# Gated linear attention in a hybrid decoder layer: score and state products of each head over its own 64 rows

## The chip, the cores and the metric

The kernel runs on one core of one Trainium2 chip. The metric is device time in microseconds (us) of one execution, as the median over runs; lower is better. TensorE multiplies matrices and writes its results to the PSUM banks, VectorE, ScalarE and GpSimd work element by element, and SyncE issues the transfers.

## What is computed

One layer over 4096 positions of width 1024, in fp32. Three groups of token mixers read the same normalised input: a gated linear recurrence (RG-LRU), gated linear attention (GLA) and a cross-attention into 256 memory tokens. Their outputs are gated with SiLU, multiplied by one output projection, added to the input and normalised. The change is in GLA alone, which has 4 heads with a key width of 64 and a value width of 128:

```python
q_dec = q * jnp.exp(cum)
k_dec = k * jnp.exp(-cum)
att = jnp.einsum("bnihk,bnjhk->bnhij", q_dec, k_dec)
att = jnp.where(causal, att, 0.0)
o_intra = jnp.einsum("bnhij,bnjhv->bnihv", att, v)
kv = jnp.einsum("bnjhk,bnjhv->nbhkv", k * jnp.exp(cum_last - cum), v)
decay = jnp.exp(cum_last[:, :, 0]).transpose(1, 0, 2, 3)
# state <- decay * state + kv, from chunk to chunk
o_inter = jnp.einsum("bnihk,nbhkv->bnihv", q_dec, s_prev)
o = (o_intra + o_inter)   # then an RMS norm per head
```

## The kernel before

The first part of the kernel goes through the sequence in 4 blocks of 1024 positions, each of two units of 512. Within a block a list gives the order of the groups of weights: `V0+G0 Q0 L0 L1 X0 L2 L3 X1 L4 V1 G1 Q1 ...`. L are RG-LRU groups, X cross-attention heads, and V, G and Q the values, gates and queries/keys of a pair of GLA heads. A second part does the output projection.

Each group issues its projections (`proj`, lines 118 to 124, with `mm3` in lines 74 to 77: three fp32r matmuls for each of 8 slices) and hands what comes after them to a generator. After each projection `tick` lets every active generator go on by one stage, in the order in which they were spawned. So the small matmuls of a generator stand between the large ones of the projections, and the order of the program on TensorE is that of these ticks.

The two heads of a pair share the 128 partitions: rows 0 to 63 belong to one, 64 to 127 to the other. `GlaQ.unit` (line 549) writes the decayed queries to `qz` with one VectorE instruction per head (line 561). `qz` has a slot of 128 columns per chunk and head, whose other 64 rows stay at the zeros written at the start (line 223). `GlaQ.post` then has, for each unit of 512 positions as 4 chunks of 128, these stages:

1. `kd`, the decayed keys (line 575), and an empty stage.
2. `pk`: four transposes of `kd`, copied to `kt_` by ScalarE (lines 587 to 591). Then `att(0)`: the scores of chunks 0 and 1 into one `pa` bank, each a matmul of 128 rows by 256 columns (both heads, line 583), and two masked copies to `attm` by VectorE (line 585).
3. `att(1)` for chunks 2 and 3, then `pkv`, the products of keys and values. These have 64 columns of weights per head and write 64 partitions each (line 599). `advance` makes the states of chunks 1 to 3 (lines 605 and 606).
4. For each half `c2` (chunks 0 and 1, then 2 and 3) one `po` bank: for each chunk and head the state product over 128 rows of `qz` (line 616) and the score product over 128 rows of `attm` (line 617). After the first half `advance(3)` writes the state for the next unit. ScalarE squares the bank (line 622), VectorE sums (624), GpSimd makes the factor (lines 69 and 71), and VectorE multiplies (626).
5. `pt`: eight transposes of the result, multiplied by the gate (lines 631 and 634).

All of these small tiles (`pk`, `pa`, `pkv`, `po`, `pt`, and those of L and X) come from the tag `aux` of the pool `ps`, four PSUM banks (lines 54 and 55). Stage 4 of a block's first unit and stage 2 of its second fall into the same tick.

Of the kernel before, what the change touches and what calls it, by code (L numbers as in the profile page):

```python
# [9 lines left out]
F32 = mybir.dt.float32  # L10
F32R = mybir.dt.float32r
BF16 = mybir.dt.bfloat16
U32 = mybir.dt.uint32
AF = mybir.ActivationFunctionType
ALU = mybir.AluOpType
# [4 lines left out]
P = 128  # L20
# [16 lines left out]
def hybrid_layer(ctx: ExitStack, tc: tile.TileContext, x, x_t, mem, mem_t, final_g,  # L37
                 w_lru, w_v0, w_oth, w_g2, w_mem, w_out, prm, out):
    nc = tc.nc
# [11 lines left out]
    def acc(name):  # L51
        return ps.tile([P, 512], F32, tag="acc", name=name)

    def aux(name):
        return ps.tile([P, 512], F32, tag="aux", name=name)
# [10 lines left out]
    def rstd_of(ss, n, cols, tag, eng=None):  # L66

        ms = small.tile([P, cols], F32, tag=tag + "m", name=tag + "m")
        (eng or nc.gpsimd).tensor_scalar(out=ms, in0=ss, scalar1=1.0 / n, scalar2=EPS, op0=ALU.mult, op1=ALU.add)
        r = small.tile([P, cols], F32, tag=tag + "r", name=tag + "r")  # L70
        nc.gpsimd.tensor_tensor(out=r, in0=ms, in1=mhalf[:, :cols], op=ALU.pow)
        return r
# [10 lines left out]
    c1 = p1.enter_context(tc.tile_pool(name="c1", bufs=1))  # L83
# [14 lines left out]
    def spawn(g):  # L98
        active.append(g)

    def big(tag, dt=F32):
        return wk.tile([P, BLK], dt, tag=tag, name=tag)
# [15 lines left out]
    def proj(o, wg, i, h, n=UNIT):  # L118

        hi, lo = wg  # L120
        hh, hl = h
        for kt in range(KT):
            s = slice(kt * P, (kt + 1) * P)
            mm3(o, hi[:, i, s], lo[:, i, s], hh[:, kt, :n], hl[:, kt, :n], kt == 0, kt == KT - 1)
# [88 lines left out]
    cmask = c1.tile([P, P], F32, name="cmask")  # L213
    make_upper_triangular(nc, cmask)
    attm = []
    for i in range(4):
        t = c1.tile([P, 2, P], F32, name=f"attm{i}")
        nc.gpsimd.memset(t, 0.0)
        attm.append(t)
    qzt = []  # L220
    for i in range(2):
        t = c1.tile([P, 4, 2, P], F32, name=f"qz{i}")
        nc.gpsimd.memset(t, 0.0)
        qzt.append(t)
    halo = cst.tile([P, 8, 3], F32, name="halo")
    nc.gpsimd.memset(halo, 0.0)
    hst = cst.tile([P, 8], F32, name="hst")
# [1 line left out]
    s_st = []  # L229
    for p in range(2):  # L230
        t = c1.tile([P, P], F32, name=f"s_st{p}")
# [54 lines left out]
    def usl(u):  # L286
        return slice(u * UNIT, (u + 1) * UNIT)

    def silu_gate(wg, i, h, sg, u):
        g = acc("gate")  # L290
        proj(g, wg, i, h)

        def post():

            nc.scalar.activation(out=sg[:, usl(u)], in_=g, func=AF.Tanh, scale=0.5)  # L295
            nc.vector.scalar_tensor_tensor(out=sg[:, usl(u)], in0=sg[:, usl(u)], scalar=1.0, in1=g,  # L296
                                           op0=ALU.add, op1=ALU.mult)
            yield 1
        spawn(post())

    def store_y(b, ct, y):
        nc.sync.dma_start(out=y_ds[b][ct], in_=y)
# [11 lines left out]
    class Lru(Group):  # L314
# [5 lines left out]
        def unit(self, u, h):  # L320
            wg = self.wg
            o = acc("u")
            proj(o, wg, 0, h)
            spawn(self.post(u, o))
            yield 1
            if self.sg is None:
                self.sg = big("sg")
            silu_gate(wg, 1, h, self.sg, u)
            yield 1
# [218 lines left out]
    class GlaQ(Group):  # L548
        def unit(self, u, h):
            g = gla[self.j]  # L550
            if "dec" not in g:
                g["dec"] = gla_decay(self.j)
            ep, em_, fs = g["dec"]
            qz = qzt[u]
            o = acc("q")
            proj(o, self.wg, 0, h)
            o3 = o.rearrange("p (s t) -> p s t", t=P)
            ep3 = ep[:, usl(u)].rearrange("p (s t) -> p s t", t=P)
            for hd in range(2):
                r = slice(hd * 64, hd * 64 + 64)  # L560
                nc.vector.scalar_tensor_tensor(out=qz[r, :, hd, :], in0=o3[r], scalar=0.125, in1=ep3[r],
                                               op0=ALU.mult, op1=ALU.mult)
            yield 1
            o = acc("k")
            proj(o, self.wg, 1, h)
            spawn(self.post(u, o))
            yield 1

        def post(self, u, o):
            p = self.j  # L570
            g = gla[p]
            ep, em_, fs = g["dec"]
            vt, sgs, qz = g["v"][u], g["sg"], qzt[u]
            kd = wk.tile([P, UNIT], F32, tag="uc", name="kd")
            nc.vector.tensor_tensor(out=kd, in0=o, in1=em_[:, usl(u)], op=ALU.mult)
            yield 1
            yield 1

            def att(c2):
                pa = aux("pa").rearrange("p (c a t) -> p c a t", c=2, a=2)  # L580
                for c in range(2):
                    s = 2 * c2 + c
                    nc.tensor.matmul(pa[:, c], kd[:, s * P:(s + 1) * P], qz[:, s], start=True, stop=True)
                for c in range(2):
                    nc.vector.copy_predicated(attm[2 * c2 + c],
                                              cmask.bitcast(U32).unsqueeze(1).broadcast_to([P, 2, P]), pa[:, c])
            pk = aux("pk")
            for s in range(4):
                nc.tensor.transpose(out=pk[:, s * P:(s + 1) * P], in_=kd[:, s * P:(s + 1) * P], identity=ident)
            kt_ = wk.tile([P, UNIT], F32, tag="t2", name="ktk")  # L590
            nc.scalar.copy(out=kt_, in_=pk)
            att(0)
            yield 1
            att(1)
            pkv = aux("pkv").rearrange("p (s d) -> p s d", d=P)
            for s in range(4):
                for hd in range(2):
                    r = slice(hd * 64, hd * 64 + 64)
                    nc.tensor.matmul(pkv[r, s, :], kt_[:, s * P + hd * 64:s * P + hd * 64 + 64],
                                     vt[:, s, hd * P:(hd + 1) * P], start=True, stop=True)  # L600
            sts = [s_st[p]] + [small.tile([P, P], F32, tag="st", name="st", bufs=3) for _ in range(3)]

            def advance(s, dst):
                sub = u * 4 + s
                nc.vector.tensor_tensor(out=dst, in0=sts[s], in1=pkv[:, s, :], op=ALU.add)
                nc.vector.tensor_scalar(out=dst, in0=dst, scalar1=fs[:, sub:sub + 1], scalar2=None, op0=ALU.mult)
            for s in range(3):
                advance(s, sts[s + 1])
            yield 1
            on = big("i").rearrange("p (a d) -> p a d", d=P)  # L610
            for c2 in range(2):
                po = aux("po").rearrange("p (a d) -> p a d", d=P)
                for c in range(2):
                    s = 2 * c2 + c
                    for hd in range(2):
                        nc.tensor.matmul(po[:, 2 * c + hd, :], qz[:, s, hd, :], sts[s], start=True, stop=False)
                        nc.tensor.matmul(po[:, 2 * c + hd, :], attm[s][:, hd, :], vt[:, s, hd * P:(hd + 1) * P],
                                         start=False, stop=True)
                if c2 == 0:
                    advance(3, s_st[p])  # L620
                sq = wk.tile([P, 4, P], F32, tag="t2", name="sq")
                nc.scalar.activation(out=sq, in_=po, func=AF.Square)
                ss = small.tile([P, 4], F32, tag="oss", name="oss")
                nc.vector.tensor_reduce(out=ss, in_=sq, op=ALU.add, axis=AX.X)
                r = rstd_of(ss, P, 4, "o")
                nc.vector.tensor_tensor(out=on[:, 4 * c2:4 * c2 + 4, :], in0=po, in1=r.unsqueeze(2).broadcast_to([P, 4, P]), op=ALU.mult)
            yield 1
            for hd in range(2):
                pt = aux("pt")
                for s in range(4):  # L630
                    nc.tensor.transpose(out=pt[:, s * P:(s + 1) * P], in_=on[:, 2 * s + hd, :],
                                        identity=ident)
                sg = sgs[hd]
                nc.vector.tensor_tensor(out=sg[:, usl(u)], in0=pt, in1=sg[:, usl(u)], op=ALU.mult)
                if u == NU - 1:
                    store_y(self.b, 8 + 2 * p + hd, sg)
            yield 1
# [283 lines left out]
    for q, (b, p, c) in enumerate(steps):  # L921
        n, _, grp, fresh = SEQ[p]
# [11 lines left out]
        for i in range(4):  # L934
            for cc in (range(NCH) if tail else [c]):
                th, tl, wh, wl = T[q - c + cc]
                for k in range(CH):
                    t = slice(i * P, (i + 1) * P)
# [78 lines left out]
```

## Time and profile before

| | us |
|---|---|
| median of 3 runs | 2636.55 |
| lowest and highest | 2634.82, 2637.12 |
| the profiled execution's own time | 2638.23 |
| its span, first to last instruction | 2636.1 |
| TensorE busy | 2581.3 (98%) |
| VectorE busy | 1686.8 (64%) |
| ScalarE busy | 1316.5 (50%) |

The profile is that of one execution. PE is TensorE's matmuls and PEld its weight loads, which run beside the matmuls; DVE is VectorE, ACT ScalarE, POOL GpSimd. A releaser (after "<-") is what ended the idle time of an engine; "issue" is idle time for which the profile shows no cause. A shape such as "128*64 128x128" is weights of 128 rows by 64 columns, then the 128 partitions by 128 columns that stream past them. The ends of matmuls are modelled and successive ones overlap, so their starts count.

### The profile page before, as it was taken

How to read it: one execution, taken by the hardware profiler on the slowest of the kernel's cores; microseconds unless marked ns; L12 is line 12 of the kernel's file. 1: busy time of each engine (PE TensorE's matmuls, PEld its weight loads, DVE VectorE, ACT ScalarE, POOL GpSimd, SP SyncE). 2: the span in 40 equal slices, each digit the busy share in tenths (PEclk: the TensorE clock that was granted, in tenths of full speed). 3: DMA queues.
4: the chain of work that ended last, by engine and by line, in shares of the span. 5: the costliest groups of instructions: out<-in, count | busy, mean ns of one | idle time of the engine just before them, and what ended most of it. 6: DMA issues, size and time to landing. Idle time of an engine off the chain costs nothing.

```text
span 2636.1 us, 33203 instructions
## 1 busy us (share of the span) xinstructions
PE 2581.3 (98%) x12954; PEld 2182.4 (83%) x12954; DVE 1686.8 (64%) x2700; ACT 1316.5 (50%) x1950; POOL 92.1 (3%) x165
## 2 busy tenths in 40 slices
PE   7999999999999999999999999999998999999997
PEld 6888888888888888888888888888887887878786
DVE  6466546665775558466546756664568587695866
ACT  6355534653664366365525744654266344353543
POOL 2000000000000000000000000000000000010100
PEclk9999999999999999999999999999999999999999
DMA  8211111331445133111212321211127456565642
GB/s 282 69 61 58 65 61 59 128 115 52 172 141 198 46 116 124 52 68 66 70 39 90 121 72 55 68 57 62 55 98 249 166 204 210 192 215 192 214 138 96
DMA packets 111597, 302.98 MB, mean 115 GB/s; under 512 B 10608, under 2 KB 11728, under 8 KB 111440
## 3 DMA queue, kind: packets, MB, share of 16 engines
q1 hardware_dynamic: 111440, 300.86, 33.5%
q8 instruction: 101, 1.65, 0.2%
q14 instruction: 56, 0.46, 0.1%
HBM read 237.91 MB, written 62.91 MB: 114 GB/s over the span
## 4 chain that ended last, share of the span: by engine, by line
PE 82%; DVE 9%; DMA 3%; ACT 3%; issue 2%; POOL 1%; SPq 0%; POOLq 0%; DVEq 0%; ACTq 0%
PE gate L75 8%; PE gate L77 8%; PE gate L76 8%; PE out L944 6%; PE out L945 6%; PE out L943 6%; PE u L77 4%; PE u L76 4%; PE u L75 4%; PE q L76 3%; PE q L75 3%; PE q L77 3%; PE vp L481 2%; PE vp L479 2%; PE vp L480 2%
## 5 line engine op out<-in xcount | busy, mean ns | idle before, releaser
L75 PE MATMUL gate<-hh,whi 128*128 128x512 f32 x1024 | 400.6, 391 | 0.0
L77 PE MATMUL gate<-hh,wlo 128*128 128x512 f32 x1024 | 398.9, 390 | 0.0
L76 PE MATMUL gate<-hl,whi 128*128 128x512 f32 x1024 | 398.6, 389 | 0.0
L943 PE MATMUL out<-wh,th 128*128 128x512 f32 x896 | 351.0, 392 | 6.8 <-ACT wh L841 6.8
L944 PE MATMUL out<-wl,th 128*128 128x512 f32 x896 | 351.4, 392 | 5.9 <-DVE wl L853 5.8
L945 PE MATMUL out<-wh,tl 128*128 128x512 f32 x896 | 350.9, 392 | 0.0
L114 DVE TENSOR_TENSOR wlo<-raw,whi 128x1024 fp32r<-128x1024 f32 (+2 forms) x152 | 191.2, 1281 | 199.8 <-ACT whi L113 170.2
L838 ACT CAST th<-B 128x1024 fp32r<-128x1024 f32 x96 | 101.1, 1053 | 281.3 <-PE out L944 281.3
L113 ACT CAST whi<-raw 128x1024 fp32r<-128x1024 f32 (+2 forms) x152 | 162.2, 1096 | 138.6 <-PE gate L76 86.5
L77 PEld LDWEIGHTS gate<-hh,wlo 128*128 128x128 f32 x1024 | 192.2, 188 | 40.4
L75 PEld LDWEIGHTS gate<-hh,whi 128*128 128x128 f32 x1024 | 192.2, 188 | 40.4 <-issue 1.5
L76 PEld LDWEIGHTS gate<-hl,whi 128*128 128x128 f32 x1024 | 192.3, 188 | 39.2
L851 DVE TENSOR_TENSOR tl<-B,th 128x1024 fp32r<-128x1024 f32 x96 | 117.5, 1224 | 144.6 <-ACT th L838 143.9
L944 PEld LDWEIGHTS out<-wl,th 128*128 128x128 f32 x896 | 169.7, 189 | 43.4 <-DVE wl L853 7.9
L943 PEld LDWEIGHTS out<-wh,th 128*128 128x128 f32 x896 | 169.6, 189 | 42.4 <-ACT wh L841 7.2
L75 PE MATMUL u<-hh,whi 128*128 128x512 f32 x512 | 203.7, 398 | 0.0
L76 PE MATMUL u<-hl,whi 128*128 128x512 f32 x512 | 199.6, 390 | 0.0
L77 PE MATMUL u<-hh,wlo 128*128 128x512 f32 x512 | 199.5, 390 | 0.0
L945 PEld LDWEIGHTS out<-wh,tl 128*128 128x128 f32 x896 | 169.6, 189 | 35.3
L337 DVE SCALAR_TENSOR_TENSOR uc<-u,prm_sb,uc 128x511 f32<-128x511 f32 (+2 forms) x192 | 143.1, 745 | 63.1 <-ACT uc L334 62.7
L296 DVE SCALAR_TENSOR_TENSOR sg<-sg,gate 128x512 f32<-128x512 f32 x128 | 86.7, 683 | 105.7 <-ACT sg L295 105.4
L295 ACT ACTIVATE sg<-gate 128x512 f32<-128x512 f32 x128 | 75.9, 600 | 152.4 <-PE gate L77 148.0
(226 smaller groups left out, 5393.0 us busy)
## 6 DMA issues: line engine op xcount, KB each, us to landing
wraw<-ws_d SPq DMA_DIRECT2D x192, 256.0 KB, 3.4
raw<-in_w_oth SPq DMA_DIRECT2D x72, 512.0 KB, 3.8
raw<-in_w_lru SPq DMA_DIRECT2D x64, 576.0 KB, 3.8
B<-y_d SPq DMA_DIRECT2D x32, 1024.0 KB, 7.3
r<-in_x SPq DMA_DIRECT2D x34, 512.0 KB, 5.2
xt<-in_x_t SPq DMA_DIRECT2D x32, 512.0 KB, 3.8
y_d<-sg SPq DMA_DIRECT2D x32, 512.0 KB, 3.2
y_d<-i SPq DMA_DIRECT2D x32, 512.0 KB, 2.6
```

Source lines behind the costliest of these rows:

```text
L75: nc.tensor.matmul(o, w_hi, r_hi, start=start, stop=False)
L76: nc.tensor.matmul(o, w_hi, r_lo, start=False, stop=False)
L77: nc.tensor.matmul(o, w_lo, r_hi, start=False, stop=stop)
L113: nc.scalar.copy(out=hi[:, i, :width], in_=raw[:, :width])
L114: nc.vector.tensor_tensor(out=lo[:, i, :width], in0=raw[:, :width], in1=hi.bitcast(F32)[:, i, :width], op=ALU.subtract)
L296: nc.vector.scalar_tensor_tensor(out=sg[:, usl(u)], in0=sg[:, usl(u)], scalar=1.0, in1=g, op0=ALU.add, op1=ALU.mult)
L337: nc.vector.scalar_tensor_tensor(out=uc[:, d:UNIT], in0=o[:, 0:UNIT - d], scalar=w, in1=uc[:, d:UNIT], op0=ALU.mult, op1=ALU.add)
L838: nc.scalar.copy(out=th, in_=t)
L851: nc.vector.tensor_tensor(out=tl, in0=t, in1=th.bitcast(F32), op=ALU.subtract)
L943: nc.tensor.matmul(o, th[:, k, t], wh[:, k], start=st, stop=False, **sk)
L944: nc.tensor.matmul(o, th[:, k, t], wl[:, k], start=False, stop=False, **sk)
L945: nc.tensor.matmul(o, tl[:, k, t], wh[:, k], start=False, stop=sp, **sk)
```

## The change

The two heads are computed over 64 rows each, and each has a bank of its own. `qz` has one slot per chunk, without zeros and without the clearing at the start, and one VectorE instruction fills it. `attm` becomes two tiles (one per head, four chunks) in place of four. All eight score products of a unit (4 chunks by 2 heads) come in one stage, each of 64 rows by 128 columns, into two `pa` banks that are held together; two masked copies follow. In the stage of `po` both banks are taken at once. For each chunk the two heads' state products, over 64 rows, come first, then the two score products over 128 rows. `advance(3)` and both heads' norms stand behind all of them.

```diff
@@ -213,15 +213,13 @@
     cmask = c1.tile([P, P], F32, name="cmask")
     make_upper_triangular(nc, cmask)
     attm = []
-    for i in range(4):
-        t = c1.tile([P, 2, P], F32, name=f"attm{i}")
+    for hd in range(2):
+        t = c1.tile([P, 4, P], F32, name=f"attm{hd}")
         nc.gpsimd.memset(t, 0.0)
         attm.append(t)
     qzt = []
     for i in range(2):
-        t = c1.tile([P, 4, 2, P], F32, name=f"qz{i}")
-        nc.gpsimd.memset(t, 0.0)
-        qzt.append(t)
+        qzt.append(c1.tile([P, 4, P], F32, name=f"qz{i}"))
     halo = cst.tile([P, 8, 3], F32, name="halo")
     nc.gpsimd.memset(halo, 0.0)
     hst = cst.tile([P, 8], F32, name="hst")
@@ -556,10 +554,7 @@
             proj(o, self.wg, 0, h)
             o3 = o.rearrange("p (s t) -> p s t", t=P)
             ep3 = ep[:, usl(u)].rearrange("p (s t) -> p s t", t=P)
-            for hd in range(2):
-                r = slice(hd * 64, hd * 64 + 64)
-                nc.vector.scalar_tensor_tensor(out=qz[r, :, hd, :], in0=o3[r], scalar=0.125, in1=ep3[r],
-                                               op0=ALU.mult, op1=ALU.mult)
+            nc.vector.scalar_tensor_tensor(out=qz, in0=o3, scalar=0.125, in1=ep3, op0=ALU.mult, op1=ALU.mult)
             yield 1
             o = acc("k")
             proj(o, self.wg, 1, h)
@@ -576,22 +571,22 @@
             yield 1
             yield 1
 
-            def att(c2):
-                pa = aux("pa").rearrange("p (c a t) -> p c a t", c=2, a=2)
-                for c in range(2):
-                    s = 2 * c2 + c
-                    nc.tensor.matmul(pa[:, c], kd[:, s * P:(s + 1) * P], qz[:, s], start=True, stop=True)
-                for c in range(2):
-                    nc.vector.copy_predicated(attm[2 * c2 + c],
-                                              cmask.bitcast(U32).unsqueeze(1).broadcast_to([P, 2, P]), pa[:, c])
+            HD = [slice(0, 64), slice(64, 128)]
             pk = aux("pk")
             for s in range(4):
                 nc.tensor.transpose(out=pk[:, s * P:(s + 1) * P], in_=kd[:, s * P:(s + 1) * P], identity=ident)
             kt_ = wk.tile([P, UNIT], F32, tag="t2", name="ktk")
             nc.scalar.copy(out=kt_, in_=pk)
-            att(0)
-            yield 1
-            att(1)
+
+            pa = [aux("pa").rearrange("p (s t) -> p s t", t=P) for _ in range(2)]
+            for s in range(4):
+                for hd in range(2):
+                    nc.tensor.matmul(pa[hd][:, s], kd[HD[hd], s * P:(s + 1) * P], qz[HD[hd], s],
+                                     start=True, stop=True)
+            for hd in range(2):
+                nc.vector.copy_predicated(attm[hd], cmask.bitcast(U32).unsqueeze(1).broadcast_to([P, 4, P]),
+                                          pa[hd])
+            yield 1
             pkv = aux("pkv").rearrange("p (s d) -> p s d", d=P)
             for s in range(4):
                 for hd in range(2):
@@ -607,28 +602,28 @@
             for s in range(3):
                 advance(s, sts[s + 1])
             yield 1
-            on = big("i").rearrange("p (a d) -> p a d", d=P)
-            for c2 in range(2):
-                po = aux("po").rearrange("p (a d) -> p a d", d=P)
-                for c in range(2):
-                    s = 2 * c2 + c
-                    for hd in range(2):
-                        nc.tensor.matmul(po[:, 2 * c + hd, :], qz[:, s, hd, :], sts[s], start=True, stop=False)
-                        nc.tensor.matmul(po[:, 2 * c + hd, :], attm[s][:, hd, :], vt[:, s, hd * P:(hd + 1) * P],
-                                         start=False, stop=True)
-                if c2 == 0:
-                    advance(3, s_st[p])
+            on = big("i").rearrange("p (h s d) -> p h s d", h=2, d=P)
+            po = [aux("po").rearrange("p (s d) -> p s d", d=P) for _ in range(2)]
+            for s in range(4):
+                for hd in range(2):
+                    nc.tensor.matmul(po[hd][:, s], qz[HD[hd], s], sts[s][HD[hd]], start=True, stop=False)
+                for hd in range(2):
+                    nc.tensor.matmul(po[hd][:, s], attm[hd][:, s], vt[:, s, hd * P:(hd + 1) * P],
+                                     start=False, stop=True)
+            advance(3, s_st[p])
+            for hd in range(2):
                 sq = wk.tile([P, 4, P], F32, tag="t2", name="sq")
-                nc.scalar.activation(out=sq, in_=po, func=AF.Square)
+                nc.scalar.activation(out=sq, in_=po[hd], func=AF.Square)
                 ss = small.tile([P, 4], F32, tag="oss", name="oss")
                 nc.vector.tensor_reduce(out=ss, in_=sq, op=ALU.add, axis=AX.X)
                 r = rstd_of(ss, P, 4, "o")
-                nc.vector.tensor_tensor(out=on[:, 4 * c2:4 * c2 + 4, :], in0=po, in1=r.unsqueeze(2).broadcast_to([P, 4, P]), op=ALU.mult)
+                nc.vector.tensor_tensor(out=on[:, hd], in0=po[hd], in1=r.unsqueeze(2).broadcast_to([P, 4, P]),
+                                        op=ALU.mult)
             yield 1
             for hd in range(2):
                 pt = aux("pt")
                 for s in range(4):
-                    nc.tensor.transpose(out=pt[:, s * P:(s + 1) * P], in_=on[:, 2 * s + hd, :],
+                    nc.tensor.transpose(out=pt[:, s * P:(s + 1) * P], in_=on[:, hd, s, :],
                                         identity=ident)
                 sg = sgs[hd]
                 nc.vector.tensor_tensor(out=sg[:, usl(u)], in0=pt, in1=sg[:, usl(u)], op=ALU.mult)
```

## Rows read from the trace of the kernel before

**Rows 1.** The page: busy time, granted clock in 40 slices, chain by engine.

```profile
PE 2581.3 (98%) x12954; PEld 2182.4 (83%) x12954; DVE 1686.8 (64%) x2700; ACT 1316.5 (50%) x1950; POOL 92.1 (3%) x165
...
PEclk9999999999999999999999999999999999999999
...
PE 82%; DVE 9%; DMA 3%; ACT 3%; issue 2%; POOL 1%; SPq 0%; POOLq 0%; DVEq 0%; ACTq 0%
```

**Rows 2.** Waits of TensorE's matmuls: us in total, times, longest us.

```profile
PE rb L169 <- POOL xr L71: 9.6, 2, 8.5
...
PE sp L415 <- DVE i L626: 1.1, 2, 0.5
```

**Rows 3.** Groups by line and shape: busy us, mean ns of one, idle before.

```profile
L616 PE MATMUL po<-st,qz 128*128 128x128 f32 x192 | 37.1, 275 | 0.0
...
L583 PE MATMUL pa<-qz,kd 128*128 128x256 f32 x128 | 32.9, 379 | 0.0
...
L616 PEld LDWEIGHTS po<-st,qz 128*128 128x128 f32 x192 | 29.2, 192 | 0.0
...
L585 DVE COPY_PREDICATED attm<-cmask,pa 128x256 f32<-128x256 uint32 x64 | 25.6, 440 | 25.0 <-PE pa L583 24.9
...
L561 DVE SCALAR_TENSOR_TENSOR qz<-q,r 64x512 f32<-64x512 f32 x32 | 21.9, 684 | 0.3
...
L599 PEld LDWEIGHTS pkv<-v,ktk 128*64 128x64 f32 x256 | 13.6, 136 | 5.3 <-issue 5.0 <-ACT uhi L407 0.3
```

**Rows 4.** The chain in order of time: start us, us, what.

```profile
124.57 0.86 PE pa L583 x4
125.43 1.02 PE pkv L599 x16
126.46 0.43 PE gate L75
126.88 0.23 PE gate L76
...
132.12 0.22 PE po L616 x2
...
135.69 0.44 PE pk L589 x4
...
142.45 0.87 PE pt L631 x8
```

**Rows 5.** Timeline of weight loads: start us, us, what, idle before.

```profile
125.36 0.85 PEld L599 LDWEIGHTS pkv<-v,ktk 128*64 128x64 f32 x16 [0.33 <-issue]
126.39 0.19 PEld L75 LDWEIGHTS gate<-hh,whi 128*128 128x128 f32 x1 [0.17 <-issue]
...
131.74 0.41 PEld L616 LDWEIGHTS po<-s_st,qz 128*128 128x128 f32 x2
132.07 0.30 PEld L617 LDWEIGHTS po<-v,attm 128*128 128x128 f32 x2
```

**Rows 6.** Timeline of ScalarE and VectorE behind the first `po`.

```profile
135.73 0.60 ACT L622 ACTIVATE sq<-po 128x512 f32<-128x512 f32 x1 [1.19 <-PE po L617]
136.22 0.58 ACT L591 COPY ktk<-pk 128x512 f32<-128x512 f32 x1
...
134.57 0.69 DVE L624 TENSOR_REDUCE oss<-sq 128x4 f32<-128x512 f32 x1 [1.14 <-ACT sq L622]
136.66 0.69 DVE L626 TENSOR_TENSOR i<-po,or 128x512 f32<-128x512 f32 x1 [1.41 <-POOL or L71]
```

**Rows 7.** Timeline of TensorE behind the second unit's `po`.

```profile
155.45 0.39 PE L617 MATMUL po<-v,attm 128*128 128x128 f32 x2
...
161.13 1.03 PE L631 MATMUL pt<-ident,i 128*128 128x128 f32 x8
```

**Rows 8.** Timeline of GpSimd at the start.

```profile
9.65 1.84 POOL L223 MEMSET qz<- 128x1024 f32 x2
...
20.11 0.42 POOL L245 TENSOR_TENSOR sc<-sc 128x8 f32<-128x8 f32 x1 [4.49 <-DVE sc L243]
```

## Prediction, made before the changed kernel had run

> **What bounds the kernel now.** I first read the busy shares and the chain of work that ended last [rows 1]: TensorE is busy for 98% of the span and makes 82% of the chain. So any time added to or taken from TensorE's stream is time of the kernel, and work of the other engines counts only where TensorE waits for it. TensorE's own waits come next [rows 2]: the longest belongs to the start, and the only one at the tiles of this change is half a microsecond, twice, where the cross-attention's `sp` waits for VectorE to have read a `po` bank. The granted clock is at nine tenths or more in all 40 slices [rows 1], so every pass here ran at the higher level, 2.4 GHz, and none of the prices is a mixture.
>
> The groups by shape [rows 3] show that each fp32 matmul leaves two records, which I call passes: the loops make 64 calls for `pa` (4 in each of 16 units), and there are 128 of them. The chain in order of time [rows 4] gives what a pass costs when others follow it: 0.22 us for two of `po`, so 0.112 each (128 columns); 0.86 for four of `pa`, so 0.215 each (256 columns); 0.87 for eight transposes `pt`, so 0.109 each. The reader should use these pitches and not the durations of 275 and 379 ns in [rows 3], because successive passes overlap.
>
> One row already shows half of the array at work: `pkv`, whose weights are 128 rows by 64 columns. Sixteen passes of 128 columns take 1.02 us there, against 16 x 0.112 = 1.79 us in full form. So two passes do run beside each other. But the row behind it takes 0.43 us where its like takes 0.23 [rows 4], and the weight loads stand still for 0.33 us ahead of `pkv` and 0.17 us behind it with no releaser but "issue" [rows 5].
>
> **The price of a stretch in half form.** From these rows: 1.02 + (0.43 - 0.23) = 1.22 us for the whole of `pkv`. Eight pairs at 0.109 are 0.87, so 0.35 us is paid for going into the other form and back. Of that one weight load of 64 columns is exposed; loads of 128 and 64 columns last 192 and 136 ns [rows 3], so 64 columns are 0.056 us. The new matmuls have 64 rows but still 128 columns, so their stretch pays 0.35 + 0.056 = 0.41 us. No row shows 64 rows by 128 columns, so this is bounded: 0 below, if the change of form is free for rows; above, both changes wait until the last pass is over by its record (275 - 109 = 166 ns each) and both loads of 128 columns lie bare (0.11 each), 0.55 us. I take 0.41, since `pkv` is the one change of form in the trace.
>
> The Trainium skill (TensorEngine Tiling (Array Packing), Key Properties) says that changing the tiling mode, as against the tile, drains the engine; the gaps around `pkv` agree. The table of the same page (Theoretical Speedup) offers up to twice the speed where the contraction is 64 or less; by that alone, halving the 27.7 us of `pa` and the 28.6 us of `po`'s state products, I estimate 2608 us.
>
> **State products in `po`.** For each of 16 units and 4 chunks, four passes of the state (two heads) lie between passes of the scores, which keep 128 rows. Before: 4 x 0.112 = 0.45 us. After: two pairs, 2 x 0.109 = 0.22, plus 0.41 to go there and back, 0.63. That is +0.18 us, 64 times: **+11.5 us**. The switch is paid for only four passes each time.
>
> **Scores `pa`, first unit of a pair.** A unit's scores were two lots of 0.865 us; now sixteen passes of 128 columns stand together: 8 x 0.109 + 0.41 = 1.28 us. Eight of the 16 units: 8 x (1.28 - 1.73) = **-3.6 us**.
>
> **Scores, second unit.** The trace puts `pk` and `pa` of the second unit right behind `po` of the first [rows 4]. There are four `aux` banks. At that point the two `po` tiles hold two, `pk` one, and one comes free from `pkv`. Before, one `pa` bank was needed there; now two are. The fourth bank must be that of `pk`, free when ScalarE has copied it, or of `po`, later still. ScalarE first has to square `po` [rows 6]: before, the copy of `pk` ended 1.11 us after `po` had left the chain (136.22 + 0.58 against 135.69); now both squares come after all of `po`, one more at 0.49 from one start to the next, so some 1.6 us. TensorE meanwhile does `pk` (0.44) and one head's passes alone; the other head's follow from about 1.65 us on, 0.87 us long, and 0.2, half the price of a stretch, to return: 2.72 - 0.44 = 2.28 us against 1.73, +0.55. If a projection's passes are fitted in between instead, two stretches are paid, 2 x (0.87 + 0.41) = 2.56, +0.83. If the bank is there at once, -0.45. I take +0.6, eight times: **+4.8 us**.
>
> **What costs nothing.** VectorE's `qz` falls from two of 684 ns to one of about 690 (a product of 128x512 takes 0.69 us [rows 6]), and four masked copies of 440 ns [rows 3] become two of between 440 and 880; VectorE is 64% busy [rows 1] and TensorE hardly waits for it [rows 2], so 0. GpSimd loses two clears at the start, 1.84 us together, and later stands idle 4.49 us for VectorE [rows 8], so 0. The squares come later: a square of 0.60 and two chains of reduction 0.69, wait for GpSimd 1.41 and product 0.69 [rows 6] end up to 0.60 + 2 x 2.79 = 6.2 us after `po`. TensorE comes back for `pt` after 6.8 us in the first unit (142.45 against 135.69 [rows 4]) and 5.5 us in the second (161.13 against 155.45 + 0.22 [rows 7]); since the first head's transposes need only the first chain, 0, or 0.7 x 8 = 6 us if that cover is gone. `advance(3)` still waits only for the first chunk's state passes, 0.
>
> **Sum:** 11.5 - 3.6 + 4.8 = +12.7 us. The profiled execution took 2638.23 us (span 2636.1), 1.7 above the median of 2636.55. It becomes 2650.9, and a median of **2649.2 us**, 0.5% slower.
>
> **Rivals.** *The switch is free for rows (faster).* If a 64-row load need not wait for the full form to run out, the 0.41 vanishes: 64 x (0.22 - 0.45) = -14.7, first units 8 x (0.87 - 1.73) = -6.9, second units 0 since their banks still keep the heads apart; 2615 us. It decides from a price of a stretch below 0.25 us, where the sum crosses zero (80 stretches). For it: two heads lie in separate halves of the rows and use separate banks, and loads normally hide behind passes. Against it: both sides of `pkv`. Chance 0.18.
>
> *The two heads' weight loads take turns.* A load of 128 columns takes about 0.11 us of the loader, as long as a pass streams, and in `po` one load follows another without a pause [rows 5], so the trace can't tell which of the two sets that pitch. If the halves can't be loaded beside each other, a state stretch lasts five pitches of 0.109 instead of three, +0.22 x 64 = +14.0, and first units gain nothing from pairs, +0.87 x 8 = +7.0: 2670.2 us. For it: `pkv` has only half the columns to load, which would hide this. Against it: `pkv`'s two halves were loaded beside each other, 16 loads in 0.85 us. Chance 0.20. The Trainium skill (TensorE: Matmul & The Clock Gate, LDWEIGHTS) says that a load's time goes by its columns and not its rows, which speaks against gaining anything on loads here; the equal 0.11 us in full form neither supports nor refutes it.
>
> *The change doesn't do what it says:* 64 rows run in full form, one head after the other. `pa` becomes 16 x 0.112 = 1.79 instead of 1.73, `po` stays: +1.0, 2637.5 us. Against it: `pkv` took its half form from its shape alone. Chance 0.12.
>
> **Chances and range.** The forecast has 0.50. A measurement of this kernel can tell about 0.2% (5.3 us) from no change. Faster by more: the free switch and a little of the forecast's cheap end, 0.20. Within: full form and cheap switches (0.18 to 0.31 us a stretch, 80 x 0.065 on either side of 0.25), 0.14. Slower: the rest, 0.66. The range of 8 in 10 runs from 2630, which takes in full form and cheap switches, to 2676, loads in turn with some of the second units at +0.83 and the late `pt`; the free switch is left out.
>
> **What would show it.** `pa` with 256 passes and `po`'s state with 256, of 64 rows; `po` of a unit 4.3 us instead of 3.58; "issue" ahead of loads 64 times more in `po`; pairs of `pa` starting together in first units, and in second units one head's passes apart from the other's. I am wrong if pairs don't start together, if loads go on through the change of form, or if TensorE stands idle for a bank for microseconds.

## The result, and the profile after

The changed kernel takes 2650.33 us in the median (2649.72 to 2650.87) against 2636.56 us: 1.0051 times the time before, with a 95% interval of 1.0039 to 1.0063. It is 13.8 us slower; 2649.2 us had been predicted. The profiled execution took 2650.35 us, with a span of 2648.6.

The page of the changed kernel says as little as that of before [rows 1]: TensorE is as busy and the chain is as much its own.

```profile
PE 2593.5 (98%) x13082; PEld 2173.6 (82%) x13082; DVE 1672.6 (63%) x2652; ACT 1316.7 (50%) x1950; POOL 95.3 (4%) x161
...
PE 81%; DVE 8%; DMA 4%; ACT 3%; issue 2%; POOL 1%; SPq 0%; POOLq 0%; DVEq 0%; ACTq 0%
```

The groups by shape answer to [rows 3]. `pa` and the state products of `po` are now of 64 rows by 128 columns.

```profile
L584 PE MATMUL pa<-qz,kd 64*128 64x128 f32 x256 | 27.8, 285 | 0.0
L609 PE MATMUL po<-st,qz 64*128 64x128 f32 x192 | 23.6, 322 | 0.0
...
L587 DVE COPY_PREDICATED attm<-cmask,pa 128x512 f32<-128x512 uint32 x32 | 21.6, 731 | 0.0
...
L557 DVE SCALAR_TENSOR_TENSOR qz<-q,r 128x512 f32<-128x512 f32 x16 | 11.0, 686 | 2.2 <-PE q L77 2.2
```

The rows that decide are in the chain in order of time, as in [rows 4]: first the scores of a first unit, then a chunk of `po`, then the second unit's scores.

```profile
117.44 0.44 PE pk L577 x4
117.88 1.09 PE pa L584 x16
118.97 0.43 PE u L75
119.40 0.23 PE u L76
...
131.32 0.42 PE po L609 x4
131.74 0.64 PE po L611 x4
132.38 0.42 PE po L609 x4
...
135.57 0.44 PE pk L577 x4
136.01 1.08 PE pa L584 x8
137.10 0.43 PE u L75
137.52 0.23 PE u L76
137.76 1.08 PE pa L584 x8
138.84 0.43 PE u L77
```

Sixteen passes of 64 rows take 1.09 us, so they do run two at a time. Eight pairs alone take 0.89, as the kernel with scores first (below) shows; the other 0.20, and 0.20 more in the pass behind them (0.43 for 0.23), are the price of going there and back, 0.40 us. In `po` four such passes take 0.42 and the four full ones behind them 0.64 instead of 0.45, so the price is the same there. In the second unit the passes of `pa` stand in two lots of eight with two projection passes between them, and so they do in all eight second units. A lot of eight takes 1.08 us, as long as the sixteen of a first unit: one head's passes alone have none to run beside. So the order on TensorE is not only that of the ticks; the kernel's text alternates the heads from product to product.

The timeline of the weight loads answers to [rows 5]: sixteen loads of 128 columns take 0.97 us, two at a time like the passes. The second head's loads in the second unit have waited for ScalarE's copy `ktk`, which they don't read: what they need is a bank, that of `pk`.

```profile
117.80 0.97 PEld L584 LDWEIGHTS pa<-qz,kd 64*128 64x128 f32 x16 [0.17 <-issue]
...
131.25 0.30 PEld L609 LDWEIGHTS po<-s_st,qz 64*128 64x128 f32 x4 [0.35 <-issue]
131.67 0.52 PEld L611 LDWEIGHTS po<-v,attm 128*128 128x128 f32 x4
...
137.69 0.96 PEld L584 LDWEIGHTS pa<-qz,kd 64*128 64x128 f32 x8 [0.36 <-ACT ktk L579]
```

ScalarE behind the first `po` answers to [rows 6]: the copy of `pk`, which frees its bank, has waited for VectorE's sum of a square.

```profile
136.79 0.59 ACT L579 COPY ktk<-pk 128x512 f32<-128x512 f32 x1 [0.32 <-DVE oss L618]
```

Which part of the execution grew can be read from the instructions of `pk` and `pt` (duration min/median/max in ns, then first and last start in us). Of the kernel before:

```profile
L589 PE MATMUL pk<-ident,kd x64: 270/272/273, 117.6 to 1859.1; 128*128 128x128 f32 x64
...
L631 PE MATMUL pt<-ident,i x128: 270/272/273, 142.3 to 1889.2; 128*128 128x128 f32 x128
```

Of the changed kernel:

```profile
L577 PE MATMUL pk<-ident,kd x64: 270/272/273, 117.3 to 1872.1; 128*128 128x128 f32 x64
...
L626 PE MATMUL pt<-ident,i x128: 270/272/273, 143.9 to 1903.7; 128*128 128x128 f32 x128
```

From the first `pk` to the last `pt` it went from 1771.6 to 1786.4 us, +14.8. Before the first `pk` 117.6 and 117.3 us pass, and behind the last `pt` 746.9 (2636.1 - 1889.2) and 744.9 us: together they are 2.3 us shorter, which is why the span grew by 12.5. The part behind the last `pt` took between 743.9 and 747.0 us in the profiles of the kernels below that keep the list of groups, so 2 us there can be scatter.

### The profile page after: what moved, and what is told of

Read it like the earlier page. It is cut to its first block, busy times and chain, and to the rows that moved or that the text cites. A ratio compares the mean times of both kernels' runs of the same rounds, so it can differ in the third digit from the quotient of the medians.

```text
span 2648.6 us, 33399 instructions
## 1 busy us (share of the span) xinstructions
PE 2593.5 (98%) x13082; PEld 2173.6 (82%) x13082; DVE 1672.6 (63%) x2652; ACT 1316.7 (50%) x1950; POOL 95.3 (4%) x161
## 4 chain that ended last, share of the span: by engine, by line
PE 81%; DVE 8%; DMA 4%; ACT 3%; issue 2%; POOL 1%; SPq 0%; POOLq 0%; DVEq 0%; ACTq 0%
PE gate L75 8%; PE gate L76 7%; PE gate L77 7%; PE out L939 6%; PE out L940 6%; PE out L938 6%; PE u L75 4%; PE u L77 4%; PE u L76 4%; PE q L75 3%; PE q L77 3%; PE q L76 3%; PE vp L479 2%; PE vp L477 2%; PE vp L478 2%; DMA x<-in_x 2%
## 5 line engine op out<-in xcount | busy, mean ns | idle before, releaser
L477 PE MATMUL vp<-whi,hh 128*128 128x272 f32 (+1 forms) x512 | 148.2, 290 | 3.0 <-ACT whi L113 2.3
```

The source lines that it names most:

```text
L477: nc.tensor.matmul(o, hh, wh, start=kt == 0, stop=False)
```

## The experiments

**Fewer stretches.** All state products of a unit come ahead of its score products. Only the first product in each bank carries the start flag.

```diff
             for s in range(4):
                 for hd in range(2):
-                    nc.tensor.matmul(po[hd][:, s], qz[HD[hd], s], sts[s][HD[hd]], start=True, stop=False)
+                    nc.tensor.matmul(po[hd][:, s], qz[HD[hd], s], sts[s][HD[hd]], start=s == 0, stop=False, ...)
+            for s in range(4):
                 for hd in range(2):
                     nc.tensor.matmul(po[hd][:, s], attm[hd][:, s], vt[:, s, hd * P:(hd + 1) * P], ...
```

> The changed kernel with all eight state products of a unit ahead of all eight score products in po, so that each unit goes into the 64-row form once for po instead of four times. Theory (each stretch in the 64-row form costs 0.41 us beside its passes): three stretches fewer in each of 16 units, 48 x 0.41 = 19.7 us less than the changed kernel, about 2630.6 us, under the kernel before; a unit's po takes 4.26 - 1.23 = 3.03 us. Rival (the change of form is free and the loss comes from the bank that the second unit waits for): the number of passes is the same, so the time stays at 2650 and po at 4.26 us.

Measured: 2632.17 us, 0.9983 times the kernel before (0.9973 to 0.9992), 18.2 us under the changed kernel. The chain in order of time:

```profile
132.65 1.09 PE po L609 x16
133.74 1.98 PE po L613 x16
135.72 0.44 PE pk L577 x4
```

A unit's `po` takes 3.07 us instead of 4.25 (131.32 to 135.57) with the same number of passes. Three stretches fewer save 1.18 us, 0.39 each. The loss in `po` comes with the number of stretches and not with the work.

**More stretches.** Each head's state product stands directly ahead of that head's score product.

```diff
                 for hd in range(2):
                     nc.tensor.matmul(po[hd][:, s], qz[HD[hd], s], sts[s][HD[hd]], start=True, stop=False)
-                for hd in range(2):
                     nc.tensor.matmul(po[hd][:, s], attm[hd][:, s], ...
```

> The changed kernel with each head's state product directly ahead of that head's score product, so that there are eight stretches of two passes per unit instead of four stretches of four. Theory (0.41 us per stretch, passes of one head one after the other at 0.11): po of a unit takes 8 x (0.22 + 0.41) + 16 x 0.112 = 6.8 us against 4.26, 16 x 2.6 = +41 us, about 2692 us. Rival (change of form free): only the pairing of the heads is lost, 64 x 0.22 = +14 us, about 2664 us.

Measured: 2689.25 us, 1.0200 times the kernel before (1.0186 to 1.0214). In the chain in order of time every two passes, of either form, cost 0.41 or 0.42 us:

```profile
130.00 0.41 PE po L609 x2
130.42 0.42 PE po L610 x2
```

A unit takes 6.67 us (130.00 to 136.67). A stretch and the scores behind it are 0.83 us, of which 0.22 + 0.22 are passes: 0.39 for the change, again. So the price goes with the number of changes, from one to eight per unit.

**Scores alone.** The queries are zero-filled again, and only `pa` uses 64 rows of them.

```diff
...
-                    nc.tensor.matmul(pa[hd][:, s], kd[HD[hd], s * P:(s + 1) * P], qz[HD[hd], s],
+                    nc.tensor.matmul(pa[hd][:, s], kd[HD[hd], s * P:(s + 1) * P], qz[HD[hd], s, hd],
...
-                    nc.tensor.matmul(po[hd][:, s], qz[HD[hd], s], sts[s][HD[hd]], start=True, stop=False)
+                    nc.tensor.matmul(po[hd][:, s], qz[:, s, hd, :], sts[s], start=True, stop=False)
```

> Only the scores pa over 64 rows and a bank for each head; the state products go over zero-filled 128 rows as in the kernel before, in the changed kernel's order. Theory: po is back at 3.57 us a unit; the scores give 8 x -0.44 in first units and 8 x +0.83 in second units, so +3.1 us on the kernel before, about 2639.7 us. Rival (the whole loss comes from the scores' second bank, and the state products cost nothing): 2650 us. Rival (loads of the two heads take turns): first units gain nothing and the sum is +6.6 us or more, 2643 us.

Measured: 2640.77 us, 1.0015 times the kernel before (1.0006 to 1.0024), +3.7 us in these runs. The chain in order of time has the full passes of `po` back, still in two banks by turns and without any price, and the second unit's two lots:

```profile
130.98 0.44 PE po L614 x4
131.43 0.45 PE po L616 x4
...
134.99 1.09 PE pa L589 x8
136.74 1.09 PE pa L589 x8
```

**State products alone.** The queries are zero-filled again, and `pa` is as in the kernel before, in its two stages; only the state products use 64 rows.

```diff
-                    nc.tensor.matmul(po[hd][:, s], qz[HD[hd], s], sts[s][HD[hd]], start=True, stop=False)
+                    nc.tensor.matmul(po[hd][:, s], qz[HD[hd], s, hd], sts[s][HD[hd]], start=True, stop=False)
...
+            att(0)
+            yield 1
+            att(1)
```

> Only the state products over 64 rows with a po bank for each head; the scores pa as in the kernel before, over 128 zero-filled rows in two stages. Theory: 64 stretches at +0.17 us, +11.0 us on the kernel before, about 2647.6 us, and no idle time or splitting at pa. Rival (the loss comes from the scores' banks): as the kernel before, 2636.6 us, or less.

Measured: 2647.16 us, 1.0040 times the kernel before (1.0026 to 1.0053), +10.1 us in these runs. Alone, the two parts cost 3.7 and 10.1 us, together 13.8: they add up. The intervals are some 2.5 and 3.5 us to either side, so that the sum fits to the tenth is chance.

**`pk` one stage earlier.** Its copy gets a buffer of its own.

```diff
             yield 1
+            pk = aux("pk")
+            ...
+            kt_ = wk.tile([P, UNIT], F32, tag="ktk", name="ktk")
+            nc.scalar.copy(out=kt_, in_=pk)
             yield 1
```

> The changed kernel with the transposes pk and their copy one stage earlier (the copy in a buffer of its own), so that the bank of pk is free again when the second unit asks for its second pa bank. Theory (the second unit's heads are kept apart by the bank of pk, which costs a second stretch and the pairing): the second unit's scores stand together as in the first, 1.30 us instead of 2.57, 8 x 1.27 = 10 us less than the changed kernel, about 2640 us. Rival (they wait for a po bank, which VectorE reads later still): the heads stay apart and the time stays at 2650 us.

Measured: 2643.49 us, 1.0023 times the kernel before (1.0014 to 1.0033), 6.8 us under the changed kernel. In the chain in order of time the second unit's passes now follow `po` in one piece:

```profile
136.77 0.64 PE po L610 x4
137.41 1.09 PE pa L583 x16
```

The edit moves `pk` and takes its copy out of the squares' buffers at once; that the bank was what the second head waited for, the row of the weight loads above says. Of the 10 us expected, 3 are missing. Part of them is a wait that grew. It fits that now two `po` and two `pa` tiles hold all four banks where the last block's cross-attention asks for one (*Without that wait*, below, takes that away). TensorE's waits in this kernel (us in total, times, longest):

```profile
PE sp L413 <- DVE i L619: 2.2, 3, 1.3
```

In the changed kernel the same row reads:

```profile
PE sp L413 <- DVE i L620: 0.9, 2, 0.5
```

Most of the rest lies ahead of the first `pa`, where nothing was to be gained. The instructions of this kernel:

```profile
L583 PE MATMUL pa<-qz,kd x256: 272/272/373, 119.2 to 1866.6; 64*128 64x128 f32 x128
...
L625 PE MATMUL pt<-ident,i x128: 270/272/273, 144.0 to 1897.3; 128*128 128x128 f32 x128
```

In the changed kernel `pa` starts at 117.8, 1.4 us sooner. From the first `pa` to the last `pt` the time went from 1785.9 to 1778.1 us, by 7.8 us; with the 1.3 us of the wait that is 9.1 of the 10.

**Both.** The edits of the first and the fifth kernel together.

> Both: all state products of a unit ahead of its score products, and pk one stage earlier. Theory (the two costs are separate terms on TensorE's stream): 48 stretches at 0.39 us, as the grouped kernel measured, and 8 x 1.27 us come off the changed kernel, 18.7 + 10.2 = 28.9 us, about 2621.5 us, 0.6% under the kernel before. Rival (with less work on TensorE another engine ends the stages, the norms behind po above all): only part of it comes, 2628 us or more, and TensorE shows waits at pt.

Measured: 2623.72 us, 0.9949 times the kernel before (0.9932 to 0.9965). Off the changed kernel come 26.6 us of the 28.9 expected; TensorE's waits have no row of `pt`. The chain in order of time:

```profile
132.14 1.09 PE po L608 x16
133.24 1.98 PE po L612 x16
135.22 1.09 PE pa L583 x16
```

**Scores first.** As both, with the score products of `po` ahead of the state products, so that two groups of 64 rows meet. The lines added:

```diff
+                    nc.tensor.matmul(po[hd][:, s], attm[hd][:, s], ..., start=s == 0, stop=False, ...)
+            for s in range(4):
+                for hd in range(2):
+                    nc.tensor.matmul(po[hd][:, s], qz[HD[hd], s], sts[s][HD[hd]], start=False, stop=True, ...)
```

> As the kernel with both, but with the score products of po ahead of the state products, so that the first unit's state products and the second unit's scores pa, all of 64 rows, follow each other directly. Theory (a stretch is paid for the change of form and not for the change of tiles): one stretch fewer in each of the 8 pairs, 8 x 0.39 = 3.1 us less than with both, about 2618.5 us, less what the first pa bank waits for the state's update on VectorE. Rival (each new group of 64-row passes pays anew): as with both, 2621.5 us.

Measured: 2621.65 us, 0.9941 times the kernel before (0.9926 to 0.9955), only 2.1 us under the kernel with both. The chain in order of time:

```profile
131.13 1.78 PE po L608 x16
132.91 1.09 PE po L612 x16
134.00 0.89 PE pa L583 x16
```

The `pa` passes cost 0.89 us here, eight pairs and nothing else: other weights, another operand and other banks in the same form pay nothing. But the last block gives some of it back. Its timeline of TensorE:

```profile
1843.64 0.39 PE L77 MATMUL q<-hh,wlo 128*128 128x512 f32 x1
1845.75 0.38 PE L413 MATMUL sp<-km_hi,uhi 128*128 128x256 f32 x1 [1.71 <-DVE i L621]
...
1847.12 0.39 PE L413 MATMUL sp<-km_hi,uhi 128*128 128x256 f32 x1 [0.39 <-DVE i L621]
...
1848.16 0.63 PE L75 MATMUL q<-hh,whi 128*128 128x512 f32 x1
1848.59 0.63 PE L76 MATMUL q<-hl,whi 128*128 128x512 f32 x1
```

TensorE stands for 2.1 us for VectorE's product `i`, which reads `po`, and soon after its passes start 0.43 us apart instead of 0.23. The busy times of that stretch (PE, PEld, DVE, ACT, POOL, then the granted clock) say why:

```profile
1847.70:1851.10 3.40, 3.40 (x11) 2.77 (x10) 2.32 (x8) 1.41 (x7) 0.00 (x0) 0.51 0.03 5
```

The kernel with both stood there too, for 1.30 and 0.39 us, but kept its clock. So against that kernel the last block loses 0.4 us by standing and, as an estimate, half of 3.4 us, 1.7, by slow passes; of the 3.1 us expected from the stretch, 1.0 is missing.

**Without that wait.** The kernel with scores first, and as a control the kernel before, with two entries of the last block's list exchanged.

```diff
-    orders.append(parse("V0+G0 Q0 L0 L1 X0 L2 L3 X1 L4 V1 G1 Q1 X2 L5 X3 L6+L7"))
+    orders.append(parse("V0+G0 Q0 L0 L1 X0 L2 L3 X1 L4 V1 G1 Q1 L5 X2 X3 L6+L7"))
```

> The fastest kernel so far (state products after score products, pk early) with X2 and L5 of the last block's list exchanged, so that no cross-attention asks for a bank while two po and two pa tiles hold all four. Theory (there TensorE stands 2.1 us for VectorE to free a po bank, and the clock is then at half speed for 3.4 us, which together hid the 3.1 us that the saved stretch gives): both vanish, 3 to 4 us less, about 2618 us. Rival (the saved stretch itself is paid elsewhere): no change, 2621.7 us.

> The kernel before with the same exchange of X2 and L5, as the control. Theory: there the wait at sp is 0.5 us and the clock does not fall, so at most 1 us less, about 2636 us. Rival (the exchange itself is worth several us): 2634 us or less.

Measured: 2616.02 us, 0.9922 times the kernel before (0.9906 to 0.9939), 5.6 us under the kernel with scores first; the control 2635.65 us, 0.9996 (0.9986 to 1.0005), no change. TensorE's waits no longer have the row of `sp` and `i`, and the granted clock is 1.00 from 1840 to 1860 us. The intervals of the two kernels with scores first overlap, but their times don't (2612.58 to 2617.87 against 2620.90 to 2623.24); that the gain is 5.6 rather than 3 to 4 us is not shown. Of the wait, 1.7 us had stood in the kernel with both as well, so not all of the gain is the stretch that had been hidden. This kernel beats both the one before and the changed one.

## Why the prediction was right

- **The bound.** TensorE's stream sets the time, as read from [rows 1]: each term found on it shows in the time. The 40 slices of [rows 1] are too coarse to say that every pass ran at the higher level: in the kernel before, the granted clock was 0.75 and 0.73 in the two stretches of 10 us from 1990 us on. But between the first `pk` and the last `pt`, where all prices were read, it was 1.00.
- **The price of a stretch.** Predicted 0.41 us from the rows of `pkv` [rows 4, 5]; measured 0.40 in the changed kernel and 0.39 in the kernels with one and with eight stretches per unit. That the 0.05 above the 0.35 of `pkv` is the load of 64 more columns, as the prediction had it, was argued; no run separates it. The Trainium skill (TensorEngine Tiling (Array Packing), Key Properties) says that changing the tiling mode, and not just the tile, drains the engine. The trace agrees for 64 rows: 0.39 us there and back, and 0.89 us for eight pairs, with nothing added, where the form stays.
- **State products.** Predicted +11.5 us; `po` of a unit took 4.25 us against 3.57, so 16 x 0.68 = +10.9. The part alone measured +10.1.
- **First units.** Predicted -3.6; `pa` took 1.09 + 0.20 = 1.29 us, 8 x (1.29 - 1.73) = -3.5.
- **Second units: the term that was mis-sized.** "I take +0.6, eight times: +4.8 us" stood between +0.55 and +0.83. Measured was the upper end: two stretches in all eight pairs, 2 x 1.28 = 2.56 against 1.73, so +6.6 us. The bank named was the right one, as `pk` one stage earlier showed. Its release was put at 1.6 us behind `po`, from ScalarE's two squares alone; it came 1.81 us behind (136.79 + 0.59 against 135.57), because the copy shares its two buffers (tag `t2`) with the squares and so also waited 0.32 us for VectorE's sum. Two projection passes stand in between; whether an earlier release would have kept them out, no run shows.
- **What was put at nothing.** VectorE's copies became 731 ns and `qz` one of 686 ns; no new wait of TensorE came of them, nor one at `pt`. The three terms give 10.9 - 3.5 + 6.6 = +14.0 of the 14.8 us between the first `pk` and the last `pt`.
- **What was luck.** That the median came within 1.1 us of the forecast: the terms were off by -0.6, +0.1 and +1.8 us, and in the profiled execution the parts that the change leaves alone came out 2.3 us shorter.
- **The rivals.** A free switch is refuted by the kernels with fewer and more stretches. Loads in turn: refuted, sixteen loads in 0.97 us. Full form: refuted, the passes run in pairs. The Trainium skill (TensorEngine Tiling (Array Packing), Theoretical Speedup) gives up to twice the speed, from which the prediction estimated 2608 us. No kernel here reaches that: the best, at 2616, has fewer changes of form but still pays for some.

## What to carry to other kernels

Two heads of 64 rows do run side by side and halve the time of their passes, but each stretch in that form costs about 0.4 us beyond its passes: with a pass of 0.112 us, saving half of each, I estimate some seven passes in a row (0.39 / 0.056) before a stretch pays. So gather all products of one form and put groups of the same form next to each other, before giving up the zero-filled rows; the same products cost +13.8 us in the order of the change and gave -20.8 us (2616.0 against 2636.8) once gathered, with `pk` one stage earlier and two list entries exchanged. And a bank held longer can be a wait or a split somewhere else, as here with that of `pk`: look at who frees the next one, and what that engine's copy itself waits for.

## What the runs showed of the hardware that was not expected

In the profile of the kernel with scores first TensorE stood for 1.71 us, worked for less than a microsecond and stood for 0.39 us more; then the granted clock was at 0.51 over 3.4 us, which is the lower of its two levels, 1.2 GHz, and passes of 512 columns went from 0.23 to 0.43 us. The wait of 0.5 us in the same place in the kernel before [rows 2] had no such sequel: passes behind it kept their pace.

How long TensorE stands doesn't decide it alone. In the same place of the kernel with both it stood for 1.69 us, and the clock stayed at 1.00 (again the stretch, its length, the busy times and the granted clock):

```profile
1845.00:1850.00 5.00, 3.31 (x29) 2.39 (x27) 2.82 (x5) 1.09 (x2) 2.40 (x4) 1.00 0.00 0
1850.00:1855.00 5.00, 5.00 (x25) 4.27 (x26) 3.79 (x12) 1.93 (x8) 0.00 (x0) 1.00 0.01 3
```

In another place of the control (the kernel before with the list exchanged) it stood for less, 1.18 us within 5, and the clock did fall:

```profile
1530.00:1535.00 5.00, 3.82 (x20) 3.08 (x19) 3.65 (x7) 1.99 (x4) 0.00 (x0) 0.86 0.07 26
1535.00:1540.00 5.00, 5.00 (x34) 5.00 (x34) 0.21 (x1) 0.37 (x1) 0.00 (x0) 0.80 0.00 0
```

What else decides stays open here.
